# One late store cut into fifteen parts of falling size in a cross-covariance attention kernel

## The chip, the cores and the metric

The kernel runs on one core of a Trainium2 chip. The metric is the device time of one execution in microseconds (us). Before the change it is 128.58 us, the median of 2 runs (128.54 to 128.63).

## The reference

For each of 8 x 12 heads, Q, K and V are 512 x 64 in float32. Q and K are normalised along the sequence, their product is a 64 x 64 matrix, a softmax runs over its rows, and V is multiplied by it:

```
Q_norm = Q / (norm(Q, axis=-2) + 1e-10)
K_norm = K / (norm(K, axis=-2) + 1e-10)
attn = einsum('bhnd,bhne->bhde', Q_norm, K_norm)
attn = exp(attn - max(attn)); attn = attn / (sum(attn) + 1e-10)
out = einsum('bhnd,bhde->bhne', V, attn)
```

The inputs are 37.75 MB and the output is 12.58 MB.

## The kernel before, in words

Four heads make a unit (HU = 4), two units make a step; there are S = 12 steps. For each step, Q and K are loaded (L183 to L187), cast to bf16 on DVE (L212), and multiplied into Gram matrices on PE (L232), which hold Q'Q, K'K and Q'K together. DVE takes the squared norms out of the diagonals (L239, L251), ACT makes the scale factors (L257, L258), POOL scales the K side (L262), PE transposes (L275), ACT takes the exponentials (L281), and DVE normalises into `ab` (L290). V is loaded (L194, L196), cast (mostly on POOL, L170), transposed on PE (L301) and copied to `vt`. PE multiplies `vt` by `ab` (L318), and ACT, in the late steps DVE too, copies the result into a store tile `so` (L166, L168).

A store tile holds 128 partitions x 2 x 512 float32: two halves (index r = 0 and 1) of 2 KB in each partition. `store(s, i)` writes one such tile of 512 KB to HBM; each step has two, so there are 24 stores. There are 13 buffers for store tiles.

The order of everything is made by a planner (`Order`, with costs and due times), which runs before the program is emitted and emits each piece in the order of its planned start. Loads and stores go to one queue, that of the sync engine SP, in the planner's order; only the first two K loads are issued by ACT. SP issues in order. Each DMA on SP takes one of eight completion semaphores in turn and, from the ninth DMA of the program on, waits first for the last DMA that used the same one. The end of SP's queue is: fourteen whole stores (L206), then the store of step 9's second tile, `FEW = (S - 3, 1)`, then the last four whole stores, of steps 10 and 11. At the end of the program SP waits for the DMAs that are still out (L493).

The store `FEW` is the only one that does not leave as one DMA. Before the change it leaves in four: of its first half the partitions 0 to 91, 92 to 99 and 100 to 127, and then its whole second half (L203, L204).

Of the kernel before, what the change touches and what calls it, by code (L numbers as in the profile page):

```python
# [102 lines left out]
def kernel(  # L103
# [7 lines left out]
    nc = tc.nc  # L111
# [50 lines left out]
    qk32, v32, vb, qkb, gram, scr, kq, n2, r8, kqs, rq, lg, ex, ab, vps, vt, po, so = ({} for _ in range(18))  # L162
# [35 lines left out]
    def store(s, i):  # L198
        o = Of[s // 2, s % 2, i].rearrange("p r (j d) -> p r j d", d=D)
        if (s, i) == FEW:  # L200

            for a, b in ((0, 92), (92, 100), (100, 128)):
                nc.sync.dma_start(out=o[a:b, 0], in_=so[s, i][a:b, 0])  # L203
            nc.sync.dma_start(out=o[:, 1], in_=so[s, i][:, 1])  # L204
            return
        nc.sync.dma_start(out=o, in_=so[s, i])  # L206

# [139 lines left out]
    for i in range(NB["ab"]):  # L347
        a = const.tile([128, HU, 2 * D], BF16, name=f"ab{i}")
# [42 lines left out]
    for u in range(U):  # L391
        s, r = divmod(u, 2)
# [21 lines left out]
    for w in range(W):  # L414
        both = 2 * w >= BOTH
        for r in range(2):
            halves = (0, 1) if (w, r) == (W - 1, 1) else (None,)
            n = 2 * w + r - NB["v"]
# [22 lines left out]
    for s in range(S):  # L441
        for x in range(4):
            i, k = divmod(x, 2)
            n = 4 * s + x - 2
            wait = [("oc", n // 4, n % 4)] if n >= 0 else []
            order = [("ou", s, x - 1) if x else back("ou", s, 1, 3)]
            piece(("ou", s, x), {"PE": 0.5}, [("vc", s // 2, *t) for t in turns(s // 2) if t[0] // 2 == k] + [("nm", s)] + wait, order, R["ou"] + 0.01 * s, outs, s, x)
            n = 2 * s + i - NB["so"]
            free = [("st", n // 2, n % 2)] if k == 0 and n >= 0 else []
            order = [("oc", s, x - 1) if x else back("oc", s, 1, 3)]  # L450
            piece(("oc", s, x), {"ACT": 0.6, "DVE": (0.68, BIAS["oc"])} if s >= BOTH else {"ACT": 0.6}, [("ou", s, x)] + free, order, R["oc"] + 0.01 * s, ocopy, s, x)
        for i in range(2):
            order = [("st", s, 0) if i else back("st", s, 1, 1)]
            piece(("st", s, i), {"DMA": X}, [("oc", s, 2 * i), ("oc", s, 2 * i + 1)], order, v_at(2 * s + i) + ST_LAG, store, s, i)
# [43 lines left out]
```

## Time and profile before

| | |
|---|---|
| Time, median of 2 runs | 128.58 us |
| Time of the profiled execution | 128.35 us |
| Its span | 126.5 us |
| DMA moved | 50.64 MB, mean 400 GB/s |
| Busy: DVE, PE, ACT, POOL | 72%, 62%, 57%, 30% of the span |
| Issue of the whole store just before `FEW` | at 109.37 us |
| Issues of the four DMAs of `FEW` | at 110.66, 111.90, 113.18, 114.49 us |
| Issues of the last four stores | from 115.81 to 119.66 us |
| Time from issue to landing, 512 KB store, median of 23 | 10.2 us |

The span runs from the first to the last instruction of the core; the time of the run has 1.85 us around it. All times on the trace's axis are from the start of the span. The row named DMA of the profile gives the mean busy share of the sixteen DMA engines in 40 equal slices of the span, in tenths; the row GB/s gives what they moved. SPq is the queue of issues of the sync engine. A row of a timeline gives the start, the duration, the engine, the line and the operation. A wait's row gives the total, the number of times and the longest, in us.

### The profile page before, as it was taken

Reading aid. Unit: us, or ns where it says so; the run is one execution under the profiler, and the core shown is the slowest. Engines: PE = TensorE matmul, PEld = TensorE weight load, DVE = VectorE, ACT = ScalarE, POOL = GpSimd, SP = SyncE. Lnnn points to the kernel's source line nnn. Section 1 sums busy time; section 2 is a strip of 40 time slices with the busy share of each in tenths; the row PEclk is TensorE's granted clock in tenths of the full one; section 3 lists DMA queues with packets and bytes.
Section 4 is the critical chain, followed back from the end, with each engine's and each line's share of the span. In section 5 each row is a group of like instructions: output and inputs, shape, how many; then the busy total and the mean of one; then the engine's idle time right before and its main releaser. Section 6 shows DMA issues by size and latency. Waiting matters only on the chain.

```text
span 126.5 us, 4885 instructions
## 1 busy us (share of the span) xinstructions
PE 78.9 (62%) x2128; PEld 64.2 (51%) x2128; DVE 90.7 (72%) x141; ACT 72.5 (57%) x220; POOL 37.4 (30%) x40
## 2 busy tenths in 40 slices
PE   0065393895964679958583999596676858473000
PEld 0054382784843568747372788484464746352000
DVE  3344749839899499899976798999999799740000
ACT  4000441539789077695883688694758969974000
POOL 4006307300745913043064303133363270300000
PEclk9999999999599555899998559959999999855555
DMA  3999999999999999999999999999999999999993
GB/s 129 408 434 411 427 413 421 413 434 408 430 417 418 409 422 417 398 414 425 422 417 412 418 419 421 416 423 423 401 415 411 402 401 407 400 407 408 405 382 149
DMA packets 15359, 50.64 MB, mean 400 GB/s; under 512 B 1130, under 2 KB 1130, under 8 KB 13930
## 3 DMA queue, kind: packets, MB, share of 16 engines
q1 hardware_dynamic: 15050, 49.29, 96.5%
q10 hardware_dynamic: 288, 1.05, 2.1%
q8 instruction: 16, 0.26, 0.7%
q14 instruction: 5, 0.04, 0.1%
HBM read 37.75 MB, written 12.58 MB: 398 GB/s over the span
## 4 chain that ended last, share of the span: by engine, by line
DVE 34%; DMA 21%; PE 19%; ACT 10%; issue 5%; POOL 2%; SPq 0%; DVEq 0%; ACTq 0%; POOLq 0%
DMA qk<-in_Q_dram 21%; DVE qkb L212 12%; PE gram L232 12%; DVE scr L239 7%; DVE ab L290 5%; ACT so L166 4%; PE po L318 3%; DVE vb L168 3%; ACT ex L281 3%; PE vps L301 3%; DVE n L251 3%; DVE vt L168 2%; ACT vt L166 2%; DVE so L168 1%; POOL kqs L262 1%
## 5 line engine op out<-in xcount | busy, mean ns | idle before, releaser
L232 PE MATMUL gram<-qkb 32*128 32x128 bf16 (+1 forms) x1504 | 36.9, 262 | 20.3 <-DVE qkb L212 7.1
L232 PEld LDWEIGHTS <-qkb 32*128 32x128 bf16 (+1 forms) x1504 | 31.0, 117 | 24.8 <-DVE qkb L212 8.9
L212 DVE CAST qkb<-qk 128x1024 bf16<-128x1024 f32 x48 | 35.3, 758 | 8.4 <-DMA qk<-in_Q_dram 6.8
L170 POOL TENSOR_SCALAR vb<-v 128x1024 bf16<-128x1024 f32 x19 | 22.0, 1169 | 43.9 <-DMA v<-in_V_dram 39.6
L166 ACT COPY so<-po 128x512 f32<-128x512 f32 x45 | 24.8, 593 | 6.6 <-PE po L318 6.5
L166 ACT COPY vt<-vps 128x1024 bf16<-128x1024 bf16 (+1 forms) x18 | 17.8, 987 | 16.5 <-PE vps L301 16.4
L318 PE MATMUL po<-ab,vt 128*64 128x128 bf16 x384 | 20.8, 252 | 5.1 <-ACT so L166 1.7
L301 PE MATMUL vps<-identb,vb 128*128 128x128 bf16 x192 | 18.4, 247 | 6.5 <-POOL vb L170 4.3
L262 POOL TENSOR_TENSOR kqs<-kq,r 64x512 f32<-64x512 f32 x12 | 14.1, 1171 | 26.7 <-ACT r L258 14.0
L239 DVE SCALAR_TENSOR_TENSOR scr<-gram,eye 64x512 f32<-64x512 f32 x24 | 16.5, 687 | 6.0 <-PE gram L232 5.8
L318 PEld LDWEIGHTS <-vt 128*64 128x64 bf16 x384 | 15.2, 127 | 9.4 <-issue 4.8
L301 PEld LDWEIGHTS <-vb 128*128 128x128 bf16 x192 | 13.5, 110 | 10.2 <-POOL vb L170 5.5
L281 ACT ACTIVATE ex<-lg,rq 128x64 f32<-128x64 f32 x48 | 14.5, 322 | 2.5 <-PE lg L275 2.3
L166 ACT COPY kq<-gram 64x512 f32<-64x512 f32 x12 | 7.0, 581 | 13.5 <-DVE scr L239 13.3
L290 DVE TENSOR_TENSOR ab<-ex,rinv 64x256 bf16<-64x256 f32 x24 | 13.4, 556 | 0.6
L281 ACT ACTIVATION_READ_ACCUMULATOR ex<-lg,rq 128x1 f32 x48 | 10.2, 213 | 0.0
L275 PE MATMUL lg<-eye,kqs 64*128 64x64 f32 x48 | 6.4, 258 | 4.3 <-POOL kqs L262 2.6
L251 DVE TENSOR_REDUCE n<-scr 128x8 f32<-128x512 f32 x12 | 8.1, 679 | 0.1
L168 DVE COPY vt<-vps 128x1024 bf16<-128x1024 bf16 (+1 forms) x8 | 7.9, 1020 | 0.1
L168 DVE CAST vb<-v 128x1024 bf16<-128x1024 f32 x5 | 7.0, 1399 | 1.3 <-DMA v<-in_V_dram 1.3
L275 PEld LDWEIGHTS lg<-eye,kqs 64*128 64x128 f32 x48 | 4.5, 156 | 6.1 <-POOL kqs L262 3.3
L287 DVE RECIPROCAL rinv<-esum 128x4 f32<-128x4 f32 x12 | 2.1, 172 | 3.4 <-ACT ex L281 3.2
(17 smaller groups left out, 16.0 us busy)
## 6 DMA issues: line engine op xcount, KB each, us to landing
out_dram<-so SPq DMA_DIRECT2D x23, 512.0 KB, 10.2
v<-in_V_dram SPq DMA_DIRECT2D x11, 1024.0 KB, 17.1
qk<-in_Q_dram SPq DMA_DIRECT2D x8, 1024.0 KB, 17.1
qk<-in_K_dram SPq DMA_DIRECT2D x8, 1024.0 KB, 17.9
qk<-in_Q_dram SPq DMA_DIRECT2D x8, 512.0 KB, 12.2
qk<-in_K_dram SPq DMA_DIRECT2D x6, 512.0 KB, 12.5
qk<-in_K_dram ACTq DMA_DIRECT2D x2, 512.0 KB
v<-in_V_dram SPq DMA_DIRECT2D x2, 512.0 KB
```

The lines of the kernel that those rows point to most:

```text
L166: nc.scalar.copy(o, i)
L168: nc.vector.tensor_copy(o, i)
L170: nc.gpsimd.tensor_scalar(out=o, in0=i, scalar1=1.0, scalar2=0.0, op0=ALU.mult, op1=ALU.add)
L212: nc.vector.tensor_copy(qkb[u][:, :, x * D:(x + 1) * D], qk32[s][:, x, r])
L232: nc.tensor.matmul(gram[s][:, h, r, 0], x, x, start=(t == 0), stop=(t == (T if u < WIDE else J) - 1))
L239: nc.vector.scalar_tensor_tensor(out=scr[s][half], in0=gram[s][half, :, :, 0, half].rearrange("p h r d -> p (h r) d"), scalar=1e-20, in1=e ...
L251: nc.vector.tensor_reduce(out=n2[s], in_=scr[s], axis=mybir.AxisListType.X, op=ALU.add)
L262: (nc.vector if eng == "DVE" else nc.gpsimd).tensor_tensor(out=kqs[s][HI], in0=kq[s][HI], in1=r8[s][HI, :, None].to_broadcast([D, 2 * HU, ...
L281: nc.scalar.activation(e[:, h, :], lg[s][:, h, :], AF.Exp, scale=rq[s][:, h:h + 1], accum_out=z[:, h:h + 1])
L290: nc.vector.tensor_tensor(out=a[half, :, half], in0=e[half], in1=ri[half, :, None].to_broadcast([D, HU, D]), op=ALU.mult,)
L301: nc.tensor.transpose(ps[:, c, n, :], vb[w][:, J * c + j].rearrange("p r d -> p (r d)"), identb)
L318: nc.tensor.matmul(po[s, x][e * D:(e + 1) * D, j].rearrange("p r d -> p (r d)"), v, ab[s][:, h, :])
```

## The change

The store `FEW` leaves in fifteen DMAs in place of four. Its first half goes in 92, 4 and 32 partitions, its second in 18, 15, 14, 13, 12, 11, 10, 9, 8, 7, 6 and 5. A packet is 2 KB, one half of one partition, before and after. The number and the order of all other DMAs stays, and so do the instructions of PE, DVE, ACT and POOL; SP has eleven DMAs more, all ahead of the last four stores. The lines below the edit move down by two.

```diff
         if (s, i) == FEW:
 
-            for a, b in ((0, 92), (92, 100), (100, 128)):
-                nc.sync.dma_start(out=o[a:b, 0], in_=so[s, i][a:b, 0])
-            nc.sync.dma_start(out=o[:, 1], in_=so[s, i][:, 1])
+            for r, cut in ((0, (92, 4, 32)), (1, (18, 15, 14, 13, 12, 11, 10, 9, 8, 7, 6, 5))):
+                a = 0
+                for n in cut:
+                    nc.sync.dma_start(out=o[a:a + n, r], in_=so[s, i][a:a + n, r])
+                    a += n
             return
         nc.sync.dma_start(out=o, in_=so[s, i])
```

## The prediction, made before the result was known

> **What bounds the kernel now.** I read the page's second part first, for whether any stage is free of the DMA bound.
>
> ```profile
> DMA  3999999999999999999999999999999999999993
> GB/s 129 408 434 411 427 413 421 413 434 408 430 417 418 409 422 417 398 414 425 422 417 412 418 419 421 416 423 423 401 415 411 402 401 407 400 407 408 405 382 149
> ```
>
> The sixteen DMA engines are full from the second slice to the last but one, so the kernel is bound by bytes. The chain of waits ends with the last copies into the store tiles, at 115.6 us; the 10.9 us after that are stores alone. Next, SP's queue, one row for each issue (start, duration), out of several short windows of the timeline:
>
> ```profile
> 109.37 0.63 SPq L206 DMA_DIRECT2D out_dram<-so  x1
> ```
> ```profile
> 110.66 0.33 SPq L203 DMA_DIRECT2D out_dram<-so  x1
> ```
> ```profile
> 111.90 0.29 SPq L203 DMA_DIRECT2D out_dram<-so  x1
> ```
> ```profile
> 113.18 0.32 SPq L203 DMA_DIRECT2D out_dram<-so  x1
> ```
> ```profile
> 114.49 0.37 SPq L204 DMA_DIRECT2D out_dram<-so  x1
> ```
> ```profile
> 119.66 0.37 SPq L206 DMA_DIRECT2D out_dram<-so  x1
> ```
>
> Each issue takes 0.3 to 0.4 us, yet they come 1.3 us apart. The waits of SP's queue say what fills the rest:
>
> ```profile
> SPq L206 <- DMA out_dram<-so: 10.1, 14, 1.0
> ...
> SPq L203 <- DMA out_dram<-so: 2.5, 3, 1.0
> ```
>
> In the program's order each DMA on SP waits for a numbered completion semaphore, and there are eight, used in turn: a DMA is issued only when the eighth before it has landed. The list of issues, for the window that holds only the store issued at 109.37, gives its time to landing:
>
> ```profile
> out_dram<-so SPq DMA_DIRECT2D x1, 512.0 KB, 10.2
> ```
>
> 109.37 + 10.2 = 119.57, and the eighth issue after it starts at 119.66. So the window of eight is what paces SP here, and it holds back a DMA of 10 KB as long as one of 512 KB. With 512 KB in each place that costs nothing, because the engines always have several us queued. Last, the table by stage for the end (the last two columns are DMA share and GB/s):
>
> ```profile
> 121.00:122.00 1.00, 0.00 (x0) 0.00 (x0) 0.00 (x0) 0.00 (x0) 0.00 (x0) 0.50 1.05 406
> 122.00:122.50 0.50, 0.00 (x0) 0.00 (x0) 0.00 (x0) 0.00 (x0) 0.00 (x0) 0.50 0.99 381
> 122.50:123.00 0.50, 0.00 (x0) 0.00 (x0) 0.00 (x0) 0.00 (x0) 0.00 (x0) 0.50 0.88 340
> 123.00:123.50 0.50, 0.00 (x0) 0.00 (x0) 0.00 (x0) 0.00 (x0) 0.00 (x0) 0.50 0.83 324
> 123.50:124.00 0.50, 0.00 (x0) 0.00 (x0) 0.00 (x0) 0.00 (x0) 0.00 (x0) 0.50 0.84 324
> 124.00:124.50 0.50, 0.00 (x0) 0.00 (x0) 0.00 (x0) 0.00 (x0) 0.00 (x0) 0.50 0.75 291
> 124.50:125.00 0.50, 0.00 (x0) 0.00 (x0) 0.00 (x0) 0.00 (x0) 0.00 (x0) 0.50 0.56 217
> 125.00:125.50 0.50, 0.00 (x0) 0.00 (x0) 0.00 (x0) 0.00 (x0) 0.00 (x0) 0.50 0.06 21
> ```
>
> The engines run out one after another from 122.3 to 125.4 us; the last packets end near 125.4, and 1.1 us later the span ends.
>
> **The change, step by step.** Call the fifteen parts p1 to p15 and the four whole stores behind them L1 to L4. Before, those places held four DMAs and L1 to L4.
>
> Bytes: the same 512 KB, in packets of 2 KB as before. Compute: no instruction of PE, DVE, ACT or POOL changes, and all their work on the stores is over at 115.6. So only SP's queue and the share of each DMA engine can move the end.
>
> Turns up to p8: p1 to p4 wait for the same semaphores as the four DMAs they replace, so 110.66, 111.90, 113.18 and 114.49 stay. p5 to p8 take the places, and the waits, of the old L1 to L4. p8 is then issued at 119.66, behind the landing of the store of 109.37. Nothing behind p8 can go earlier, since SP issues in order. L1, which before went at 115.81, now stands behind eight more issues.
>
> Turns from p8 to L1: p9 waits for p1. The trace's completion records show the 92-partition DMA finishing on four engines only, at 118.42, 118.85, 119.22 and 119.68 us, so it is there before p9's turn at about 120.0. p10 to p15 wait for p2 to p7, issued by 118.4 and each only a few packets behind p1; they cost no wait either. SP then runs at its own pace. The rows for 92, 8 and 28 partitions are 0.33, 0.29 and 0.32 us, mean 0.31, and between two issues on SP without a wait lie 0.05 (from 32.20 for 0.37 to the next at 32.62). Eight issues, p8 to p15, at 0.36 are 2.9 us: L1 starts at 122.56. The lower end is 0.34 each (2.7); the upper is the program's first six issues on SP, from 0.74 to 3.27 us, 0.5 apart: 4.0. I take 0.36, from rows of the same queue, stage and kind of transfer. L1 also waits for p8, which has had 2.9 us by then.
>
> Start of data: at the start of the program the engines are idle too. SP's first load is issued at 0.74, the table by stage has 0 GB/s up to 1.70 and 205 in 1.70:1.80, so 1.0 us from issue to data. That is a load, and L1 is a store, for which no row shows it. The lower end is 0.4, the time that a store's issue itself takes; the upper is 1.35, since ACT's first load, issued at 0.73, has its first packet in the trace at 2.08. I take 1.0, the nearer row (the same queue), and 0.1 for engines that start later than the first. L1 moves from 123.65 on.
>
> What is left in the engines by then: between the store of 109.37 and L1 lie 200 partitions of p1 to p8 and 56 of p9 to p15, 0.5 MB, 1.3 us at the 408 GB/s of this stage, and the engines that run ahead today are through with theirs earlier still. All are empty before 122. So the cover that hid SP's pace is gone, and the spread between engines is gone with it: L1 to L4 start on all sixteen at once, 2.10 MB / 408 GB/s = 5.14 us. L2 to L4 follow at 0.42 us each (0.37 and 0.05), well within the 1.29 us that each store takes (0.524 MB / 408 GB/s), and wait for p9 to p11, issued over 2 us before.
>
> Sum: 119.66 + 2.9 + 1.0 + 0.1 + 5.14 = 128.8 us for the last packet, against 125.4: +3.4. The 1.1 us behind it stay. Span 126.5 + 3.4 = 129.9; the profiled execution's time, 128.35, becomes 131.75. It stood 0.23 under the median of the runs, so against 128.58 the forecast is 132.0 us.
>
> **Shares, and a rule against a row.** The completion records show 4 completions for 92 partitions, 8 for 8 and 14 for 28; four of the 8 come 0.2 us behind those of the 92, so it is the same engines that come first each time. Counted by such divisors, the four engines of the 92 get 23 + 1 + 2 + 2 + 11 = 39 packets in place of 23 + 1 + 2 + 8 = 34, and the least loaded gets 2 in place of 8.
>
> The Trainium skill, "DMA: Bandwidth & Descriptors", section "Why a DMA increments its semaphore by 16 and not by 1", says that a DMA from SP uses the largest number of engines up to 16 that divides its slowest dimension, the lowest-numbered ones. Read by itself, with no eye for the window of eight, it would price the change as rival A below, 129.0, because it speaks of shares and not of turns; by the rows above it is 132.0. The same page, section "Latency and other measured facts", gives some 0.6 us to a first byte on this path, where the row has 1.0; by it the sum would be 131.6.
>
> **Rivals.**
> A, the pause is hidden and only the uneven shares count. Then it is five more packets on four engines, one of which ends last today (75 packets of 0.08 us behind the 92's last completion of 119.68 are 125.7, where L4 lands: 119.66 + 6.0), at 2 KB / (408 / 16 GB/s) = 0.08 us, 0.4 us: 129.0. For it: the queue is over 6 us deep at 119.66 today (L4 lands 6.0 after its issue). Against: that depth is L1 to L3, which are no longer ahead of the wait. It needs L1 issued by about 118.7, 1.0 before the last engine runs dry behind the store of 109.37.
>
> B, not slower: the parts don't hold SP back, because the small DMAs give their semaphores back as fast as they are issued. Then p5 to p15 follow p4 at 0.36 each, L1 at 114.49 + 0.36 x 12 = 118.8, data at 119.9, and all engines start level: last packet at 125.0, 0.4 earlier, 128.2. The spread it removes is worth 1.2 at most (the shares missing in the last seven rows, each half a us), 127.4. It decides where L1 goes before 119.2 (122.56 - 3.4). Against: p5 to p8 wait for 512 KB stores, whatever their own size.
>
> C, slower still: issues cost the 0.5 us of the program's start, +1.1: 133.1; or p8's landing takes over 2.9 us, from which point every us counts in full.
>
> D, the parts of prime size don't spread: 13, 11, 7 and 5 on one engine each would be 36 packets, 2.9 us, on one engine. Begun at about 120.5, that ends at 123.4, when L1's data begins: 132.0 to 132.5.
>
> **How the numbers follow.** The forecast (with D's small variation) gets 0.79, A 0.07, B 0.03, C 0.11. The forecast's own range is 131.2 (0.34 an issue, -0.2, and 0.4 to the data, -0.6) to 132.5 (1.35 to the data, or D); C carries the upper end to 133.2. So 131.2 to 133.2, which leaves out A, B and the far end of C. A measurement here tells about 2% from no change, 126.0 to 131.15: slower by over 2% is the forecast nearly whole, C and D, 0.88; within 2% is A, nearly all of B and a forecast at its lower edge, 0.11; faster, 0.01.
>
> **What would show it.** Right: in the profile after, p8 is issued near 119.7 and L1 near 122.6; the parts from p9 on come 0.36 apart; DMA falls to nearly nothing between 121 and 123.6 and is then full for 5.1 us and stops on all engines together, with no slope. Up to 119.6 the rows are those of before. Wrong: L1 issued before 119.2; no hole in the DMA row; a sloping end; or issues of the parts at 0.5 us or more.

## The result and the profile after

The changed kernel takes 132.22 us (median of 2 runs, 132.18 to 132.25) against 128.58: a ratio of 1.0282, 95% interval 1.0238 to 1.0326. The forecast was 132.0 in 131.2 to 133.2. Its profiled execution has a span of 130.5 us and a time of 132.25.

The two rows of the page that answer to those before, DMA share in tenths and GB/s in 40 slices:

```profile
DMA  4999999999999999999999999999999999995295
GB/s 99 404 436 409 426 413 417 418 436 404 431 426 418 408 412 428 400 415 432 426 406 413 413 431 411 426 426 406 409 413 405 399 406 400 406 392 218 67 406 213
```

The same full row as before, but now with a hole in the 37th and 38th slice (117.5 to 124 us). SP's queue, from two short windows of the timeline: p8, then p15 and the first whole store behind the parts, L1 (the parts are issued by line L205, the whole stores by L208). Below them the table by stage of the end.

```profile
119.94 0.30 SPq L205 DMA_DIRECT2D out_dram<-so  x1
```
```profile
122.42 0.29 SPq L205 DMA_DIRECT2D out_dram<-so  x1
122.82 0.40 SPq L208 DMA_DIRECT2D out_dram<-so  x1
```
```profile
119.00:120.00 1.00, 0.00 (x0) 0.00 (x0) 0.00 (x0) 0.00 (x0) 0.00 (x0) 0.50 0.55 197
120.00:121.00 1.00, 0.00 (x0) 0.00 (x0) 0.00 (x0) 0.00 (x0) 0.00 (x0) 0.50 0.13 31
121.00:122.00 1.00, 0.00 (x0) 0.00 (x0) 0.00 (x0) 0.00 (x0) 0.00 (x0) 0.50 0.24 62
122.00:123.00 1.00, 0.00 (x0) 0.00 (x0) 0.00 (x0) 0.00 (x0) 0.00 (x0) 0.50 0.15 43
123.00:123.50 0.50, 0.00 (x0) 0.00 (x0) 0.00 (x0) 0.00 (x0) 0.00 (x0) 0.50 0.09 25
123.50:124.00 0.50, 0.00 (x0) 0.00 (x0) 0.00 (x0) 0.00 (x0) 0.00 (x0) 0.50 0.53 209
124.00:125.00 1.00, 0.00 (x0) 0.00 (x0) 0.00 (x0) 0.00 (x0) 0.00 (x0) 0.50 1.03 399
...
128.50:129.00 0.50, 0.00 (x0) 0.00 (x0) 0.00 (x0) 0.00 (x0) 0.00 (x0) 0.50 0.85 324
129.00:129.50 0.50, 0.00 (x0) 0.00 (x0) 0.00 (x0) 0.00 (x0) 0.00 (x0) 0.50 0.00 0
```

From 120.0 to 123.5 the engines move only what is left of the first parts and what each later part brings as it is issued. L1 to L4 then run at full rate and stop within half a us; the slope from 122.3 to 125.4 us of the kernel before is gone. The waits of SP's queue show no wait for p9 to p15 and only eight for the parts, p1 to p8:

```profile
SPq L205 <- DMA out_dram<-so: 7.3, 8, 1.0
```

### The profile page after: what moved, and what is told of

Read it like the earlier page. It is cut to its first block, busy times and chain, and to the rows that moved or that the text cites. A ratio compares the mean times of both kernels' runs of the same rounds, so it can differ in the third digit from the quotient of the medians.

```text
span 130.5 us, 4896 instructions
## 1 busy us (share of the span) xinstructions
PE 78.6 (60%) x2128; PEld 63.3 (49%) x2128; DVE 93.3 (72%) x141; ACT 72.1 (55%) x220; POOL 35.8 (27%) x40
## 4 chain that ended last, share of the span: by engine, by line
DVE 35%; DMA 27%; PE 11%; ACT 10%; issue 4%; POOL 1%; DVEq 0%; POOLq 0%
DMA qk<-in_Q_dram 19%; DVE qkb L214 15%; DMA qk<-in_K_dram 8%; PE gram L234 7%; DVE scr L241 6%; DVE ab L292 5%; ACT vt L166 4%; ACT so L166 3%; DVE vb L168 3%; PE vps L303 3%; DVE vt L168 2%; ACT ex L283 2%; DVE n L253 2%; DVE so L168 2%; ACT kq L166 1%
## 5 line engine op out<-in xcount | busy, mean ns | idle before, releaser
L234 PE MATMUL gram<-qkb 32*128 32x128 bf16 (+1 forms) x1504 | 36.1, 257 | 23.3 <-DVE qkb L214 8.0
L234 PEld LDWEIGHTS <-qkb 32*128 32x128 bf16 (+1 forms) x1504 | 30.1, 115 | 28.2 <-DVE qkb L214 10.5
L214 DVE CAST qkb<-qk 128x1024 bf16<-128x1024 f32 x48 | 37.2, 799 | 8.7 <-DMA qk<-in_Q_dram 7.3
L170 POOL TENSOR_SCALAR vb<-v 128x1024 bf16<-128x1024 f32 x19 | 20.9, 1113 | 43.3 <-DMA v<-in_V_dram 34.2
L303 PE MATMUL vps<-identb,vb 128*128 128x128 bf16 x192 | 20.3, 263 | 4.8 <-POOL vb L170 3.4
L320 PE MATMUL po<-ab,vt 128*64 128x128 bf16 x384 | 19.3, 243 | 5.9 <-issue 3.1
L303 PEld LDWEIGHTS <-vb 128*128 128x128 bf16 x192 | 14.7, 118 | 8.9 <-POOL vb L170 4.7
L320 PEld LDWEIGHTS <-vt 128*64 128x64 bf16 x384 | 13.7, 122 | 10.0 <-issue 5.8
L292 DVE TENSOR_TENSOR ab<-ex,rinv 64x256 bf16<-64x256 f32 x24 | 15.2, 634 | 0.6
L168 DVE CAST vb<-v 128x1024 bf16<-128x1024 f32 x5 | 5.9, 1187 | 0.1
```

What stands on the lines that cost most here:

```text
L168: nc.vector.tensor_copy(o, i)
L170: nc.gpsimd.tensor_scalar(out=o, in0=i, scalar1=1.0, scalar2=0.0, op0=ALU.mult, op1=ALU.add)
L214: nc.vector.tensor_copy(qkb[u][:, :, x * D:(x + 1) * D], qk32[s][:, x, r])
L234: nc.tensor.matmul(gram[s][:, h, r, 0], x, x, start=(t == 0), stop=(t == (T if u < WIDE else J) - 1))
L292: nc.vector.tensor_tensor(out=a[half, :, half], in0=e[half], in1=ri[half, :, None].to_broadcast([D, HU, D]), op=ALU.mult,)
L303: nc.tensor.transpose(ps[:, c, n, :], vb[w][:, J * c + j].rearrange("p r d -> p (r d)"), identb)
```

## The experiments

Theory T: the window of eight DMAs holds p8 back to the landing of an earlier store, SP's turns behind it hold L1 back, and the engines run dry. A turn is the time from one issue of SP to its next. Rival S: the loss comes from the uneven shares of the engines. A third reading: each small DMA costs something, wherever it stands. The edits are shown against the changed kernel, by their main lines. Ratios are against the kernel before on the same chip (128.46 or 128.47 us there), with 95% intervals.

**The number of parts, with even shares.** Two kernels keep the shares of before and change the number of DMAs only, to eleven and to seven:

```diff
-            for r, cut in ((0, (92, 4, 32)), (1, (18, 15, 14, 13, 12, 11, 10, 9, 8, 7, 6, 5))):
+            for r, cut in ((0, (92, 8, 28)), (1, (16,) * 8)):
+            for r, cut in ((0, (92, 8, 28)), (1, (32,) * 4)):
```

Eleven: 

> The store leaves in eleven DMAs: first half in 92, 8 and 28 partitions as before, second half in eight of 16, so that every engine gets the shares that it had before and only the number of DMAs grows. Theory T (the window of eight and SP's pace make the pause): the eighth DMA is issued at 119.7 us, three more follow at 0.36, the first whole store behind them goes at 119.7 + 4 x 0.36 = 121.1, last packet near 122.0 + 5.3 = 127.3, time 128.58 + 1.9 = 130.5 us (130.1 to 130.9). Rival S (uneven shares of the engines make the loss): the shares are those of before, 128.6 us.

Measured: 130.85 us, ratio 1.0181 (1.0160 to 1.0202). p8 and p9, then L1, in SP's queue:

```profile
119.88 0.32 SPq L205 DMA_DIRECT2D out_dram<-so  x1
```
```profile
120.24 0.42 SPq L205 DMA_DIRECT2D out_dram<-so  x1
```
```profile
121.69 0.40 SPq L208 DMA_DIRECT2D out_dram<-so  x1
```

S falls: with the shares of before, 2.4 us are lost. The time is 0.35 over T's. L1 goes 0.55 later than T had it (121.69 against 121.14): 0.2 of that is a p8 that comes later, and 0.4 are the turns. Three of the four took 0.46 to 0.52 in place of 0.36, since the issue of a part of 16, which has sixteen completions in the trace, took 0.42 us without a wait.

Seven: 

> The store leaves in seven DMAs: 92, 8 and 28 partitions, then four of 32, shares as before. Theory T: the first whole store behind them waits for the store of 109.4 us and goes at 119.7 itself, without any part behind the eighth turn; data at 120.6, last packet 120.6 + 5.3 = 125.9, time 128.58 + 0.5 = 129.1 us (128.7 to 129.3). Rival S: 128.6 us. A cost for each DMA regardless of the window (3.64 us for eleven more DMAs, 0.33 each, three more here): 129.6 us.

Measured: 129.26 us, ratio 1.0064 (1.0050 to 1.0078). L1 takes p8's place, and even so the engines run dry for half a us:

```profile
119.69 0.40 SPq L208 DMA_DIRECT2D out_dram<-so  x1
```
```profile
119.50:120.00 0.50, 0.00 (x0) 0.00 (x0) 0.00 (x0) 0.00 (x0) 0.00 (x0) 0.50 0.59 217
120.00:120.50 0.50, 0.00 (x0) 0.00 (x0) 0.00 (x0) 0.00 (x0) 0.00 (x0) 0.50 0.04 12
120.50:121.00 0.50, 0.00 (x0) 0.00 (x0) 0.00 (x0) 0.00 (x0) 0.00 (x0) 0.50 0.77 303
```

The loss is 0.8 us, closer to T's 0.5 than to S's nothing; a fixed cost for each DMA, 1.0, is as near, and this run alone does not exclude it.

**More parts.** The number taken to twenty-three, with small parts on few engines:

```diff
+            for r, cut in ((0, (92, 4, 32)), (1, (8,) * 12 + (4,) * 8)):
```

> The store leaves in 23 DMAs: 92, 4 and 32 partitions, then twelve of 8 and eight of 4, each on eight engines or four. Theory T: behind the eighth DMA, still issued near 119.7 us, stand fifteen more before the first whole store; parts on eight engines or fewer were issued in 0.29 us plus 0.045, so the first whole store goes at 119.7 + 16 x 0.34 = 125.1, 2.3 to 2.6 later than in the changed kernel, and the time is 132.2 + 2.4 = 134.6 us (134.2 to 135.1). If the loss came with the first few parts and were fixed: 132.2 us.

Measured: 134.62 us, ratio 1.0481 (1.0465 to 1.0497). p8 is issued at 119.68, and L1 at

```profile
125.14 0.40 SPq L208 DMA_DIRECT2D out_dram<-so  x1
```

as expected to 0.1 us. Four kernels now give L1's issue, and the end of the last packet by the trace: 119.69 and 125.91 (seven), 121.69 and 127.91 (eleven), 122.82 and 129.04 (fifteen), 125.14 and 131.36 (twenty-three). The difference is 6.22 us in each to 0.01, with even shares and uneven ones: in these four, L1's issue sets the end. Their times alone would also fit a cost of about 0.3 us for each DMA; the runs below that move the parts or the stores decide between the two.

**The shares, with the number of before.** Four DMAs that load the first four engines nearly as the fifteen do, by the count of completions:

```diff
+            for r, cut in ((0, (92, 36)), (1, (100, 28))):
```

> The store leaves in four DMAs as before, but in 92, 36, 100 and 28 partitions, which by the divisors 4, 12, 10 and 14 gives the first four engines 23 + 3 + 10 + 2 = 38 packets of 2 KB (39 in the changed kernel, 34 before) and the last two none. Theory T: no turn is added, so no pause; only four packets of 0.08 us more on the engines that end last, 128.58 + 0.3 = 128.9 us (128.6 to 129.1). Rival S: nearly the loss of the whole change, 131.5 to 132 us.

Measured: 128.71 us, ratio 1.0018 (1.0009 to 1.0027), +0.2. The last store is issued at 119.61, as before, and the engines' slope only becomes longer by a few packets (before, the row 125.00:125.50 had 21 GB/s and the next 0):

```profile
125.00:125.50 0.50, 0.00 (x0) 0.00 (x0) 0.00 (x0) 0.00 (x0) 0.00 (x0) 0.50 0.20 78
125.50:126.00 0.50, 0.00 (x0) 0.00 (x0) 0.00 (x0) 0.00 (x0) 0.00 (x0) 0.50 0.03 12
```

So shares like those of the fifteen cost some tenths of a us, as the prediction had it under rival A, and they are not what the change costs.

**One half of the change alone.** The first half's new cut, with a whole second half:

```diff
+            for r, cut in ((0, (92, 4, 32)), (1, (128,))):
```

> Only the first half's part of the change: 92, 4 and 32 partitions in place of 92, 8 and 28, the second half whole, four DMAs. Theory T: no turn is added; the shares go from 34, 11, 10 and 8 packets to 34, 10, 10 and 10, which lengthens none of the engines that end last: 128.5 us (128.3 to 128.7), no difference from before. If the first half's cut had a share in the loss, some tenths above that.

Measured: 128.39 us, ratio 0.9995 (0.9986 to 1.0004). At an equal number of DMAs, the first half's cut has no part in the loss.

**Twelve of the parts from another queue.** The twelve parts of the second half issued by POOL:

```diff
+            for r, cut, eng in ((0, (92, 4, 32), nc.sync), (1, (18, 15, 14, 13, 12, 11, 10, 9, 8, 7, 6, 5), nc.gpsimd)):
...
+                    eng.dma_start(out=o[a:a + n, r], in_=so[s, i][a:a + n, r])
```

> The same fifteen parts; the twelve of the second half are issued by POOL, which has been idle since its last scaling and whose DMAs use semaphores of their own, so SP has the three of the first half and the four whole stores. Theory T: SP's turns are as before the change or earlier (one DMA fewer ahead of the last stores, the first of them at 114.5 us, the last at 118.4), the engines never run dry, 128.7 us (128.3 to 129.3), as long as POOL's twelve issues, for which no row has a price, are over by about 123 us. A cost of each small DMA wherever it is issued: 132 us. Rival S cannot be told apart here, since which engines POOL's parts use isn't known.

Measured: 129.02 us, ratio 1.0042 (1.0027 to 1.0057). POOL issues twelve in 7.6 us, about 0.5 each, beside SP's turns, and the last whole store goes at 118.81:

```profile
109.69 4.21 POOL L205 DMA_DIRECT2D out_dram<-so  x8 [1.06 <-ACT so L166]
115.01 1.61 POOL L205 DMA_DIRECT2D out_dram<-so  x3 [1.10 <-DMA out_dram<-so]
116.83 0.50 POOL L205 DMA_DIRECT2D out_dram<-so  x1 [0.20 <-issue]
```
```profile
119.00:122.00 3.00, 0.00 (x0) 0.00 (x0) 0.00 (x0) 0.00 (x0) 0.00 (x0) 0.50 1.06 402
```

No hole: 402 GB/s from 119 to 122, most of which is empty in the changed kernel, with the same fifteen parts. The third reading, wherever the DMAs are issued, falls here: 0.6 us are left of 3.6. For parts that SP issues, the next run decides. Where these 0.6 lie was not tried. The last packet ends at 125.84, 0.45 later than before, and it is one of SP's queue (POOL's were over at 121.99); the shares could give that, but which engines POOL's parts used is not known.

**The parts among the stores.** Same parts and shares on SP, four parts at a time between the whole stores (`few(4)` issues the next four of `rest`):

```diff
+                    rest.append((o[a:a + n, r], so[s, i][a:a + n, r]))
...
+            few(4)
             return
         nc.sync.dma_start(out=o, in_=so[s, i])
+        if rest:
+            few(4)
```

> The same fifteen parts with the same shares as in the changed kernel, but the four whole stores stand between them: four parts, a store, four parts, a store, four, a store, three, the last store. Theory T: two whole stores are issued by 120.4 us and cover most of the turns; the third goes near 122.6 and the last near 123.7 (its turn comes behind the landing of the second), last packet near 126.2, time 128.58 + 0.8 = 129.4 us (128.9 to 130.0). Rival S, or a cost for each small DMA wherever it stands: the time of the changed kernel, 132.2 us.

Measured: 130.31 us, ratio 1.0144 (1.0129 to 1.0158): half of the loss is gone, but not as much as expected. The four whole stores:

```profile
116.04 0.40 SPq L216 DMA_DIRECT2D out_dram<-so  x1
```
```profile
120.67 0.39 SPq L216 DMA_DIRECT2D out_dram<-so  x1
```
```profile
123.08 0.39 SPq L216 DMA_DIRECT2D out_dram<-so  x1
```
```profile
124.83 0.39 SPq L216 DMA_DIRECT2D out_dram<-so  x1
```
```profile
121.00:121.50 0.50, 0.00 (x0) 0.00 (x0) 0.00 (x0) 0.00 (x0) 0.00 (x0) 0.50 0.30 78
...
123.00:123.50 0.50, 0.00 (x0) 0.00 (x0) 0.00 (x0) 0.00 (x0) 0.00 (x0) 0.50 0.34 94
123.50:124.00 0.50, 0.00 (x0) 0.00 (x0) 0.00 (x0) 0.00 (x0) 0.00 (x0) 0.50 0.08 29
```

One store of 512 KB covers 1.3 us, and between the second and the third lie 2.4 us, with four parts in them. The expectation overlooked the hole ahead of 121.5 and had the last two stores 0.5 and 1.1 us too early. One reason lies in the issues: behind a whole store they took longer than in the changed kernel. The parts of 11 and 10 behind the second store took 0.41 and 0.73 us (0.35 and 0.33 in the changed kernel), those of 7 and 6 behind the third 0.35 and 0.46 (0.29 each). Even so, the same fifteen parts on SP with the same shares cost half as much when they stand elsewhere in the queue, which neither S nor the third reading allows.

**The stores from another queue.** The fifteen parts stay on SP; ACT issues the last four stores:

```diff
+    last4 = []
...
+        if s >= S - 2:
+            last4.append((o, so[s, i]))
+            if (s, i) == (S - 1, 1):
+                for o, x in last4:
+                    nc.scalar.dma_start(out=o, in_=x)
+            return
```

> The same fifteen parts on SP with the same shares, but the last four whole stores are issued by ACT, behind its last copy (115.6 us). The eight semaphores are shared, and given in the program's order: the first whole store waits for the store issued at 109.4, the second for part 3, the third for part 6, the last for part 8. Theory T: the whole stores no longer stand behind SP's turns; the first goes at 119.7, the last near 121.2, data from 120.6 without a hole, last packet near 126.0, time 128.58 + 0.7 = 129.3 us (128.9 to 129.8). If the parts cost by their number or their shares, and not by what they hold up: 132 us.

Measured: 130.48 us, ratio 1.0152 (1.0138 to 1.0165), a miss by 1.2. The first and the last of the four stores (ACTq is the queue of ACT's issues) went at

```profile
119.60 0.44 ACTq L214 DMA_DIRECT2D out_dram<-so  x1
```
```profile
121.69 1.22 ACTq L214 DMA_DIRECT2D out_dram<-so  x1
```

where 119.7 and 121.2 were expected, so the stores did get past the parts and 1.6 of the change's 3.6 us came back. But there was a hole of 1 us (29 GB/s in 119.50:120.50; "without a hole" was wrong, since a store that is issued at 119.6 has data only 0.9 to 1.0 later, as in the kernel with seven), and now the parts were late in their turn: the issues of four of them, from 120.78 on, took SP 0.8 to 1.3 us each, and the fifteenth went at

```profile
125.08 0.36 SPq L207 DMA_DIRECT2D out_dram<-so  x1
```

By the trace's packets, those of ACT's stores ended at 126.70 and those of the parts at 126.87, so the late parts stand alone only in the last 0.2 us; how much they slowed the stores before that was not settled. Nor was it settled why SP's issues grew so long. ACT's presence alone is not shown to be the reason: the last of the four began at 123.89, when ACT's issues were over (122.91), and long issues behind whole stores came in the run above with SP alone.

## Why the prediction was right

*Turns up to p8.* Expected at 119.66, measured 119.94. The store at 109.37 before is at 109.69 after: the whole run is 0.3 us late from before the change's place on (the first of the fourteen stores is at 92.82 before and 93.15 after). That is 0.3 us that the sum did not have. It is there before the edited store, so it is not the change's; the traces of the other kernels have the store ahead of the parts anywhere from 109.28 to 109.63.

*Turns from p8 to L1.* Expected eight at 0.36, 2.9 us; measured 122.82 - 119.94 = 2.88. p9 found p1 landed with 0.2 us to spare (p1's last completion is at 120.05, p9's issue at 120.28). The kernels with eleven and twenty-three parts moved L1 with their number of turns. That 0.36 fitted so well is in part luck. It came from parts that had waited for their semaphores, while the turns here were from 0.34 to 0.40; with parts of 16 they were 0.46 to 0.52, for which the sum had no term.

*Start of data.* Expected 1.0 us from a load on SP; the trace has L1's first packet at 123.74, 0.92 after its issue. The Trainium skill, "DMA: Bandwidth & Descriptors", section "Latency and other measured facts", gives about 0.6. It does not say from which moment it counts. From the start of the issue, as the sum counts, this run has 0.92 and speaks for the row; from the issue's end (122.82 + 0.40) it has 0.52.

*L1 to L4.* Expected 0.1 + 5.14; from the first packet to the end of the last are 5.30 us (123.74 to 129.04). From there to the span's end, 130.47 by the trace, are 1.4 us, where the sum had 1.1; the cause stays open.

*All engines empty before 122.* Not quite: they moved 25 to 62 GB/s to 123.5, as the parts came in. What had been queued up to p7 was gone by 120.4, the last packet of p15 ended at 123.52 and L1's began at 123.74, so the consequence, all sixteen starting on L1 at once, held.

*Rivals.* A had the mechanism of the shares right and its size nearly (0.4 expected with 39 packets; 0.2 measured with 38, and 0.4 at the last packet of the two traces), but the pause is not hidden. B is excluded by L1 at 122.82. When POOL issued twelve of the parts they did not hold SP back, as B supposed, and even then 0.6 was lost, not gained. D did not occur: the trace's completion records have thirteen completions from its data for the part of 13 partitions, so a prime size is spread too. C's dear issues did not occur: the parts from p9 on took 0.29 to 0.35.

The prediction was right in its steps. Against the profiled execution's own time the sum gave 131.75 and the run took 132.25; the 0.5 are the 0.3 by which the run was late and the 0.3 at the span's end, less 0.1 around the span (1.78 in place of 1.85). That the medians agree to 0.2 is partly luck: the sum added 0.23 because the profiled execution before lay that far under its median, and the one after lies 0.03 above its own. What the sum says of the change, from p8's issue at 119.94 to the last packet at 129.04, is right to 0.1 us: 9.1 both ways.

## What to carry to other kernels

Where a queue allows a fixed number of DMAs in flight, count its depth in bytes and not in DMAs: eight places filled with 10 to 36 KB hold at most 0.29 MB, 0.7 us at the 408 GB/s of this stage, and everything behind them in the queue then waits at the issuer's pace. A cut that makes a transfer's shares finer is priced first by the turns it adds ahead of large transfers (here nothing for the first half's cut at an equal number, 0.34 to 0.52 us for each part from the eighth on), and only then by the shares (0.2 us here). If many small DMAs are needed, an idle engine with semaphores of its own can issue them: here that cost 0.6 us in place of 3.6.

## What the runs showed of the hardware that was not expected

In the kernels with eleven, fifteen and twenty-three DMAs, the issue of a part on SP, without a wait ahead of it, took 0.29 us for 4 to 8 partitions (the first of them 0.30), 0.31 for 9, 0.33 for 10, 0.35 for 11 and 0.42 for 16. In the first two of these kernels they have as many completions in the trace as partitions; above eight, each one more took about 0.016 to 0.02 us. A part of 16 that had waited for its semaphore took 0.32. Behind a whole store some took far longer: 0.73 for 10 partitions in the kernel with the parts among the stores.

Of four whole stores issued one behind the other, the first two took 0.40 and 0.41 us, the third 0.70 and the fourth 1.11, alike in the kernels with seven, eleven, fifteen and twenty-three DMAs. With three stores queued ahead of the last, that cost nothing: the end stayed 6.22 us behind L1.
